# A 3x3 convolution with residual on one core: first image load and first residual load at the fronts of two engines' programs

## The chip, the cores and the metric

The kernel runs on one core of a Trainium2 chip. Its engines are PE (TensorE, matmuls), DVE (VectorE), ACT (ScalarE), POOL (GpSimd) and SP (SyncE, which here only issues DMAs). Each engine runs its own program in order; semaphores tie them together. The metric is the device time of one execution in microseconds (us); a lower time is better.

## The reference

Sixteen images of 64 channels and 64 x 64 pixels, all float32, are convolved with a 64 x 64 x 3 x 3 weight at padding 1, and a residual of the output's shape is added:

```
x_pad = np.pad(x, ((0, 0), (0, 0), (1, 1), (1, 1)))
for b, co, ci, kh, kw:
    output[b, co] += weight[co, ci, kh, kw] * x_pad[b, ci, kh:kh+64, kw:kw+64]
return output + residual
```

## The kernel before

**Data.** Images go in pairs: pair p (0 to 7) is images 2p and 2p+1, whose 128 channels fill the 128 partitions. One load or store of a pair is 128 rows of 16,384 bytes, 2,048 KB. `xr` has three buffers for image pairs as they come from memory, `ro` eight, one for each pair, which take the residual, are added to in place and are stored as the output. `xp` has four buffers for single images in bfloat16, even rows of pixels in partitions 64 to 127 and odd rows in partitions 0 to 63, so that one matmul with 128 rows handles two rows of the kernel at once. `ps` is two PSUM buffers, one image each. `wraw` holds the weights as loaded, 64 rows (output channels) of 2,304 bytes; `wl` holds them transposed, in bfloat16, in the six blocks that the matmuls use.

**The order is written by hand**, an engine at a time:

- SP (L120 to L130) loads, for each pair, the images (`load_x`, L71) and the residual (`load_ro`, L74). From pair 3 on it first waits until ACT has taken the images of the pair three before out of `xr` (L123, semaphore `s_half`). Then it issues five stores (`store`, L77), each once DVE's adds have got so far (L129, `s_add`). All these transfers are on SP's one DMA queue. The last three stores (L217) follow when everything else is done.
- The very first image load is taken out of its place by `to_the_front` (L99) and put into SP's program ahead of the drain at which all engines meet at the start, so it is issued at 0.00.
- ACT issues the load of the weights (L151) on its own DMA queue, and then makes two casts per image from `xr` to `xp` (L159, L163). The first cast of a pair waits for the pair's load.
- POOL writes a 64 x 64 identity for the transposes (L133, L135) and zeros the borders of `xp` and the empty blocks of `wl`.
- PE waits for the identity and the weights (L191, L192), makes nine transposes of 64 x 64 weights into PSUM (L195), one for each position in the 3x3 kernel, and then, for each image, 24 matmuls in six groups of four (L206, recorded at L83 where weights are loaded and L84 where not). Per image it waits for a free PSUM buffer (`s_bank`) and for the image's second cast (`s_pack`).
- DVE waits for the transposes (L166), makes six casts from PSUM into `wl` (L172), and then two adds per image (L182), `ro` = `ps` + `ro`. The first add of a pair waits for the pair's residual (L180: `s_r[p]`, a semaphore for each pair); the first of an image waits for its convolution (`s_conv`). `s_add` rises with an image's first add, so it counts images whose first add is done.

The time from the program's start to the first matmul of L83 therefore takes: the first image load and its casts on one side, the load of the weights, the transposes and DVE's casts on the other.

Of the kernel before, what the change touches and what calls it, by code (L numbers as in the profile page):

```python
# [8 lines left out]
FP32 = mybir.dt.float32  # L9
# [6 lines left out]
def kernel(  # L16
# [7 lines left out]
    nc = tc.nc  # L24
# [6 lines left out]
    NPIX = H * W  # L31
    NPAIR = B // 2
# [3 lines left out]
    NXR = 3  # L36
# [3 lines left out]
    res_bc = residual.rearrange("b c h w -> (b c) (h w)")  # L40
    out_bc = out.rearrange("b c h w -> (b c) (h w)")
    x_bc = x.rearrange("b c h w -> (b c) (h w)")
    w_flat = weight.rearrange("co ci kh kw -> co (ci kh kw)")

    pool = ctx.enter_context(tc.tile_pool(name="pool", bufs=1))
    psum = ctx.enter_context(tc.tile_pool(name="psum", bufs=1, space=bass.MemoryType.PSUM))

    ident = pool.tile([64, 64], FP32)
    ro = [pool.tile([128, NPIX], FP32, name=f"ro{p}") for p in range(NPAIR)]
    xr = [nc.alloc_sbuf_tensor(f"xr{i}", [128, NPIX], FP32) for i in range(NXR)]  # L50

    xp = [pool.tile([128, J + 1, W], BF16, name=f"xp{i}") for i in range(NXP)]
    wraw = nc.alloc_sbuf_tensor("wraw", [64, 576], FP32)
    wl = pool.tile([128, 2, 3, 2, 64], BF16)
    ps = [psum.tile([128, NCHUNK, JC, W], FP32, name=f"ps{i}") for i in range(2)]

    sem = lambda name: tc.alloc_semaphore(name)
    s_w = sem("s_w")
    s_x = [sem(f"s_x{i}") for i in range(NXR)]
    s_r = [sem(f"s_r{p}") for p in range(NPAIR)]  # L60
    s_out = sem("s_out")
    s_id = sem("s_id")
    s_wt = sem("s_wt")
# [4 lines left out]
    s_add = sem("s_add")  # L68

    def load_x(p):  # L70
        return nc.sync.dma_start(out=xr[p % NXR][:, :], in_=x_bc[128 * p : 128 * p + 128, :]).then_inc(s_x[p % NXR], 16)  # L71

    def load_ro(p):
        nc.sync.dma_start(out=ro[p][:, :], in_=res_bc[128 * p : 128 * p + 128, :]).then_inc(s_r[p], 16)  # L74

    def store(p):
        return nc.sync.dma_start(out=out_bc[128 * p : 128 * p + 128, :], in_=ro[p][:, :])  # L77

    def matmul(out_, lhsT, rhs, start, stop, ldweights):

        e = nc.tensor
        if ldweights:
            return e.matmul(out=out_, lhsT=lhsT, rhs=rhs, start=start, stop=stop, skip_group_check=True)  # L83
        return e.add_instruction(  # L84
            mybir.InstMatmult(
                name=nc.get_next_instruction_name(),
                engine=PE,
                ins=[e.lower_ap(rhs), e.lower_ap(lhsT)],
                outs=[e.lower_ap(out_)],
                start_tensor_calc=start,  # L90
                stop_tensor_calc=stop,
                tile_size=(128, 128),
                tile_position=(0, 0),
                bass_skip_group_check=True,
                ldweights=False,
            )
        )

    def to_the_front(dma):  # L99

        def fixed(ap):
            t = ap.bass_ap.tensor.name
            return mybir.PhysicalAccessPattern(
                ap=ap.ap, offset=ap.bass_ap.offset, dtype=ap.dtype, memref=t, memsetref=t + "_set", bass_ap=ap.bass_ap
            )

        front = nc.main_func.blocks[0].instructions
        here = nc.cur_bb.bb.instructions  # L110
        ins = here.pop()
        assert ins.name == dma.ins.name
        at = next(
            i for i, e in enumerate(front) if e.engine == mybir.EngineType.SP and isinstance(e, mybir.InstDrain)
        )
        front.insert(at, copy.replace(ins, ins=[fixed(a) for a in ins.ins], outs=[fixed(a) for a in ins.outs]))

    with tc.tile_critical(no_gpsimd_drain=True):  # L118

        for p in range(NPAIR):  # L120
            if p >= NXR:

                nc.sync.wait_ge(s_half, 2 * (p - NXR) + 3)  # L123
            i = load_x(p)
            if p == 0:
                to_the_front(i)
            load_ro(p)
        for p in range(NEARLY):
            nc.sync.wait_ge(s_add, 2 * p + 3)  # L129
            store(p).then_inc(s_out, 16)  # L130


        nc.gpsimd.memset(ident[:, :], 0.0).then_inc(s_id, 1)  # L133
        nc.gpsimd.wait_ge(s_id, 1)
        nc.gpsimd.affine_select(  # L135
            out=ident[:, :],
            in_=ident[:, :],
            compare_op=mybir.AluOpType.not_equal,
            fill=1.0,
            base=0,  # L140
            pattern=[[-1, 64]],
            channel_multiplier=1,
        ).then_inc(s_id, 1)
        for t in xp:
            nc.gpsimd.memset(t[0:64, 0, :], 0.0).then_inc(s_id, 1)  # L145
            nc.gpsimd.memset(t[64:128, J, :], 0.0).then_inc(s_id, 1)  # L146
        nc.gpsimd.memset(wl[0:64, 0, :, 1, :], 0.0).then_inc(s_id, 1)  # L147
        nc.gpsimd.memset(wl[64:128, 1, :, 0, :], 0.0).then_inc(s_id, 1)  # L148


        nc.scalar.dma_start(out=wraw[:, :], in_=w_flat[:, :]).then_inc(s_w, 16)  # L151
        for n in range(B):
            p, im = divmod(n, 2)
            hp = slice(64 * im, 64 * im + 64)
            x4 = xr[p % NXR].rearrange("q (j two w) -> q j two w", two=2, w=W)
            t = xp[n % NXP]
            if im == 0:
                nc.scalar.wait_ge(s_x[p % NXR], 16 * (p // NXR + 1))
            i = nc.scalar.copy(out=t[64:128, 0:J, :], in_=x4[hp, :, 0, :])  # L159
            i.then_inc(s_half, 1)  # L160
            if n >= NXP:
                i._wait_ge(s_conv, n - NXP + 1)
            nc.scalar.copy(out=t[0:64, 1 : J + 1, :], in_=x4[hp, :, 1, :]).then_inc(s_pack, 1)  # L163


        nc.vector.wait_ge(s_wt, 1)  # L166
        tpf = ps[0].rearrange("p c j w -> p (c j) w")

        blocks = ((0, 0, 0, 0), (1, 0, 0, 1), (1, 0, 1, 0), (0, 1, 0, 2), (0, 1, 1, 1), (1, 1, 1, 2))
        for half, d, par, kh in blocks:  # L170
            hp = slice(64 * half, 64 * half + 64)
            i = nc.vector.tensor_copy(out=wl[hp, d, :, par, :], in_=tpf[0:64, 3 * kh : 3 * kh + 3, :])  # L172
        i.then_inc(s_bank, 2)
        for n in range(B):
            p, im = divmod(n, 2)
            hp = slice(64 * im, 64 * im + 64)
            o4 = ro[p].rearrange("q (j two w) -> q j two w", two=2, w=W)
            psj = ps[n % 2].rearrange("q c j w -> q (c j) w")
            if im == 0:
                nc.vector.wait_ge(s_r[p], 16)  # L180
            for par in range(2):
                i = nc.vector.tensor_tensor(  # L182
                    out=o4[hp, :, par, :], in0=psj[64 * par : 64 * par + 64, :, :], in1=o4[hp, :, par, :], op=ADD
                )
                if par == 0:
                    i._wait_ge(s_conv, n + 1)

                i.then_inc(s_add if par == 0 or n == B - 1 else s_bank, 1)


        nc.tensor.wait_ge(s_id, 4 + 2 * NXP)  # L191
        nc.tensor.wait_ge(s_w, 16)  # L192
        wraw3 = wraw.rearrange("p (ci t) -> p ci t", t=9)
        for t in range(9):
            i = nc.tensor.transpose(out=ps[0][0:64, t // 8, t % 8, :], in_=wraw3[:, :, t], identity=ident[:, :])  # L195
        i.then_inc(s_wt, 1)
        with nc.Fori(0, B // NXP, 1, engines=[PE]):
            for n in range(NXP):
                nc.tensor.wait_ge(s_bank, 1).then_inc(s_bank, -1)
                nc.tensor.wait_ge(s_pack, 1).then_inc(s_pack, -1)  # L200
                order = [(1, 0), (1, 1), (0, 0), (0, 1), (2, 0), (2, 1)]
                for i, (kw, d) in enumerate(order):
                    xlo, xhi = max(0, 1 - kw), min(W, W + 1 - kw)
                    for c in range(NCHUNK):
                        j0 = JC * c
                        m = matmul(  # L206
                            ps[n % 2][:, c, :, xlo:xhi],
                            wl[:, d, kw, :, :].rearrange("q r c -> q (r c)"),
                            xp[n][:, j0 + d : j0 + d + JC, xlo + kw - 1 : xhi + kw - 1],
                            i == 0,  # L210
                            i == len(order) - 1,
                            c == 0,
                        )
                m.then_inc(s_conv, 1)
# [36 lines left out]
```

## Time and profile before

| what | us |
|---|---|
| median of 3 executions | 124.26 (124.14 to 124.42) |
| the profiled execution, its own time | 124.16 |
| its span, first to last instruction | 122.1 |
| PE busy | 86.5 |
| DVE busy | 75.2 |
| ACT busy | 62.0 |
| first cast of ACT starts | 8.89 |
| first cast of image pair 1 starts (image 2) | 18.71 |
| DVE's first add starts | 20.98 |
| SP issues the image loads of pairs 3 to 7 at | 20.63, 30.48, 40.27, 50.06, 59.87 |

Times in the span are counted from its first instruction. The page cuts the span into 40 slices of 3.05 us: a digit is the busy share in tenths, and the row GB/s is what all DMA engines moved. A line of the groups gives the source line, engine, operation, what is written and read, the count, the busy time and the mean duration in ns, and the idle time before with what ended it. A line of the timeline gives the start, the duration, the engine, the line and the count; "q" behind an engine's name is its sequencer, which issues DMAs. A line of the windows gives the stretch, its length, the busy time of PE, weight loads, DVE, ACT and POOL, the granted PE clock, the DMA share and GB/s.

### The profile page before, as it was taken

The page shows a single profiled execution, that of the slowest core. Times are in us where ns is not written, and L with a number is a line of the kernel's source. Part 1 is how long each engine was busy: PE and PEld are TensorE (multiplying, and loading weights), DVE is VectorE, ACT ScalarE, POOL GpSimd, SP SyncE. Part 2 cuts the span into 40 slices and gives each one's busy share as a digit, 9 for nine tenths or more (in the row PEclk, how much of TensorE's full clock was granted, in tenths as well). Part 3 has the DMA queues.
Part 4 walks back from the last instruction along what each step waited for, and adds up shares of the span by engine and source line. Part 5 has one row for each costly group of instructions (what it writes and reads, how often), then busy time and mean ns, then how long its engine had stood idle before and what let it go on. Part 6 is the DMA issues. An engine that isn't in the chain of part 4 may idle for free.

```text
span 122.1 us, 729 instructions
## 1 busy us (share of the span) xinstructions
PE 86.5 (71%) x389; PEld 10.4 (9%) x105; DVE 75.2 (62%) x38; ACT 62.0 (51%) x33; POOL 2.2 (2%) x16
## 2 busy tenths in 40 slices
PE   0003799999999999999999999999999930000000
PEld 0003000101111010101010101111110100000000
DVE  0004101989889898898989889898798988000000
ACT  4009948966984993992994896699000000000000
POOL 5100000000000000000000000000000000000000
PEclk9999999999999999999999999999999999555555
DMA  6999999999999999999999999999999999999993
GB/s 182 408 348 429 429 429 429 429 424 429 429 429 424 429 429 429 429 429 429 429 429 419 429 429 424 429 429 429 435 435 435 429 429 429 435 435 429 429 429 140
DMA packets 3536, 50.48 MB, mean 413 GB/s; under 512 B 400, under 2 KB 400, under 8 KB 464
## 3 DMA queue, kind: packets, MB, share of 16 engines
q1 hardware_dynamic: 3456, 50.33, 97.8%
q10 hardware_dynamic: 80, 0.15, 0.4%
HBM read 33.70 MB, written 16.78 MB: 413 GB/s over the span
## 4 chain that ended last, share of the span: by engine, by line
PE 70%; DVEq 2%; DVE 2%; issue 0%
PE ps L84 53%; PE ps L83 17%; DVEq L118 2%; DVE ro L182 2%
## 5 line engine op out<-in xcount | busy, mean ns | idle before, releaser
L182 DVE TENSOR_TENSOR ro<-ps,ro 64x2048 f32<-64x2048 f32 x32 | 73.2, 2289 | 17.4 <-PE ps L84 16.9
L84 PE MATMUL ps<-xp,wl 128*128 128x504 bf16 (+1 forms) x288 | 79.9, 387 | 0.2
L159 ACT CAST xp<-xr 64x2048 bf16<-64x2048 f32 x16 | 30.3, 1896 | 21.3 <-DMA xr<-in_x_dram 21.1
L83 PE MATMUL ps<-xp,wl 128*128 128x504 bf16 (+1 forms) x92 | 35.6, 387 | 2.4 <-PEq L200 2.4
L163 ACT CAST xp<-xr 64x2048 bf16<-64x2048 f32 x16 | 30.4, 1897 | 0.4
L83 PEld LDWEIGHTS ps<-xp,wl 128*128 128x128 bf16 x96 | 9.5, 99 | 77.5 <-issue 77.5
L172 DVE CAST wl<-ps 64x192 bf16<-64x192 f32 x6 | 1.9, 347 | 10.9 <-PE ps L195 10.8
L195 PE MATMUL ps<-ident,wraw 64*64 64x64 f32 x9 | 1.1, 305 | 9.6 <-DMA wraw<-in_weight_dram 9.6
L159 ACT ACT_TABLE_LOAD x1 | 1.3, 1283 | 1.5 <-SPq L118 1.5
L195 PEld LDWEIGHTS ps<-ident,wraw 64*64 64x64 f32 x9 | 0.9, 163 | 9.6 <-issue 9.6
L146 POOL MEMSET xp<- 64x64 bf16 x4 | 0.6, 147 | 0.2
L145 POOL MEMSET xp<- 64x64 bf16 x4 | 0.6, 145 | 0.2
L148 POOL MEMSET wl<- 64x192 bf16 x1 | 0.3, 253 | 0.1
L147 POOL MEMSET wl<- 64x192 bf16 x1 | 0.3, 252 | 0.1
L135 POOL TENSOR_SCALAR_AFFINE_SELECT ident<-ident 64x64 f32<-64x64 f32 x1 | 0.2, 233 | 0.2 <-POOL ident L133 0.2
L133 POOL MEMSET ident<- 64x64 f32 x1 | 0.1, 145 | 0.5 <-SPq L118 0.5
L235 POOL MEMSET const-bfloat16-1.0<- 128x1 bf16 x1 | 0.1, 113 | 0.0
L235 POOL MEMSET const-uint8-127<- 128x1 uint8 x1 | 0.1, 112 | 0.0
L235 POOL MEMSET const-float32-1.0<- 128x1 f32 x1 | 0.1, 109 | 0.0
L235 POOL MEMSET const-float32-0.0<- 128x1 f32 x1 | 0.1, 104 | 0.2 <-issue 0.2
## 6 DMA issues: line engine op xcount, KB each, us to landing
xr<-in_x_dram SPq DMA_DIRECT2D x8, 2048.0 KB, 17.6
ro<-in_residual_dram SPq DMA_DIRECT2D x8, 2048.0 KB, 22.1
out_dram<-ro SPq DMA_DIRECT2D x8, 2048.0 KB, 28.7
wraw<-in_weight_dram ACTq DMA_DIRECT2D x1, 144.0 KB, 8.5
```

What stands on the lines that cost most here:

```text
L83: return e.matmul(out=out_, lhsT=lhsT, rhs=rhs, start=start, stop=stop, skip_group_check=True)
L84: return e.add_instruction(mybir.InstMatmult(name=nc.get_next_instruction_name(), engine=PE, ins=[e.lower_ap(rhs), e.lower_ap(lhsT)], outs ...
L118: with tc.tile_critical(no_gpsimd_drain=True):
L145: nc.gpsimd.memset(t[0:64, 0, :], 0.0).then_inc(s_id, 1)
L146: nc.gpsimd.memset(t[64:128, J, :], 0.0).then_inc(s_id, 1)
L147: nc.gpsimd.memset(wl[0:64, 0, :, 1, :], 0.0).then_inc(s_id, 1)
L159: i = nc.scalar.copy(out=t[64:128, 0:J, :], in_=x4[hp, :, 0, :])
L163: nc.scalar.copy(out=t[0:64, 1 : J + 1, :], in_=x4[hp, :, 1, :]).then_inc(s_pack, 1)
L172: i = nc.vector.tensor_copy(out=wl[hp, d, :, par, :], in_=tpf[0:64, 3 * kh : 3 * kh + 3, :])
L182: i = nc.vector.tensor_tensor(out=o4[hp, :, par, :], in0=psj[64 * par : 64 * par + 64, :, :], in1=o4[hp, :, par, :], op=ADD)
L195: i = nc.tensor.transpose(out=ps[0][0:64, t // 8, t % 8, :], in_=wraw3[:, :, t], identity=ident[:, :])
L235: nc = _bacc.Bacc("TRN2", target_bir_lowering=False, num_devices=1)
```

## The change

The residual load of pair 0 leaves SP's program and goes to the front of ACT's, ahead of ACT's drain, as the first image load is in SP's. The load of the weights leaves ACT's program; SP issues it in the place where residual 0 was, behind the first image load and on the same queue. The weights now lie as 16 rows of 9,216 bytes (four output channels to a partition), so PE makes 36 transposes of 16 rows by 64 columns, with a 16 x 16 identity. There are three residual semaphores instead of eight; since one is used again for pair p when it was used for pair p-3, SP now waits before the residual load of pair p (3 to 7) until the first add of image 2(p-3) is done. To be addressed ahead of the drain, `ro0` is allocated as `xr` is.

```
-    ident = pool.tile([64, 64], FP32)
-    ro = [pool.tile([128, NPIX], FP32, name=f"ro{p}") for p in range(NPAIR)]
+    ident = pool.tile([16, 16], FP32)
+    ro = [nc.alloc_sbuf_tensor("ro0", [128, NPIX], FP32)]
+    ro += [pool.tile([128, NPIX], FP32, name=f"ro{p}") for p in range(1, NPAIR)]
...
-    wraw = nc.alloc_sbuf_tensor("wraw", [64, 576], FP32)
+    wraw = nc.alloc_sbuf_tensor("wraw", [16, 4, 576], FP32)
...
-    s_r = [sem(f"s_r{p}") for p in range(NPAIR)]
+    s_r = [sem(f"s_r{i}") for i in range(NXR)]
...
-    def load_ro(p):
-        nc.sync.dma_start(out=ro[p][:, :], in_=res_bc[128 * p : 128 * p + 128, :]).then_inc(s_r[p], 16)
+    def load_ro(p, engine=nc.sync):
+        return engine.dma_start(out=ro[p][:, :], in_=res_bc[128 * p : 128 * p + 128, :]).then_inc(s_r[p % NXR], 16)
...
-            i for i, e in enumerate(front) if e.engine == mybir.EngineType.SP and isinstance(e, mybir.InstDrain)
+            i for i, e in enumerate(front) if e.engine == ins.engine and isinstance(e, mybir.InstDrain)
...
             if p == 0:
                 to_the_front(i)
-            load_ro(p)
+                nc.sync.dma_start(out=wraw[:, :, :], in_=w_flat.rearrange("(q u) f -> q u f", u=4)).then_inc(s_w, 16)
+            if p >= NXR:
+
+                nc.sync.wait_ge(s_add, 2 * (p - NXR) + 1)
+            if p > 0:
+                load_ro(p)
...
-            pattern=[[-1, 64]],
+            pattern=[[-1, 16]],
...
-        nc.scalar.dma_start(out=wraw[:, :], in_=w_flat[:, :]).then_inc(s_w, 16)
+        to_the_front(load_ro(0, nc.scalar))
...
-                nc.vector.wait_ge(s_r[p], 16)
+                nc.vector.wait_ge(s_r[p % NXR], 16 * (p // NXR + 1))
...
-        wraw3 = wraw.rearrange("p (ci t) -> p ci t", t=9)
+        wraw4 = wraw.rearrange("q u (ci t) -> q u t ci", t=9)
         for t in range(9):
-            i = nc.tensor.transpose(out=ps[0][0:64, t // 8, t % 8, :], in_=wraw3[:, :, t], identity=ident[:, :])
+            for u in range(4):
+                i = nc.tensor.transpose(
+                    out=ps[0].rearrange("p c j (q u) -> p (c j) u q", u=4)[0:64, t, u, :],
+                    in_=wraw4[:, u, t, :],
+                    identity=ident[:, :],
+                )
```

## The prediction

> **What bounds the kernel now.** I read the page first (engine shares, the 40 slices, the chain), then the windows of half a microsecond over the start, then the timelines of SP, ACT and DVE, and last the end.
>
> ```profile
> DMA  6999999999999999999999999999999999999993
> GB/s 182 408 348 429 429 429 429 429 424 429 429 429 424 429 429 429 429 429 429 429 429 419 429 429 424 429 429 429 435 435 435 429 429 429 435 435 429 429 429 140
> PE 70%; DVEq 2%; DVE 2%; issue 0%
> L195 PE MATMUL ps<-ident,wraw 64*64 64x64 f32 x9 | 1.1, 305 | 9.6 <-DMA wraw<-in_weight_dram 9.6
> ...
> 9.63 1.14 PE L195 MATMUL ps<-ident,wraw 64*64 64x64 f32 x9 [9.63 <-DMA wraw<-in_weight_dram]
> 10.81 1.97 DVE L172 CAST wl<-ps 64x192 bf16<-64x192 f32 x6 [10.81 <-PE ps L195]
> 10.81 1.90 ACT L163 CAST xp<-xr 64x2048 bf16<-64x2048 f32 x1
> 13.12 0.58 PE L83 MATMUL ps<-xp,wl 128*128 128x512 bf16 x1 [2.35 <-PEq L200]
> ...
> 98.78 4.61 DVE L182 TENSOR_TENSOR ro<-ps,ro 64x2048 f32<-64x2048 f32 x2 [0.58 <-PE ps L84]
> 103.68 1.76 SPq L77 DMA_DIRECT2D out_dram<-ro  x3
> ```
>
> The DMA engines never rest, and the chain of waits runs almost wholly over PE: two bounds, nearly equal. The DMA side: 50.48 MB at 429 GB/s is 117.7 us. Of this the loads, the weights and the first five stores (44.2 MB) take 103 us; counting bytes to 10 us in the windows, the stream behaves as if it ran at full rate from about 2.4 us, so they are done near 105.3. The compute side: PE starts at 13.12, the first image takes 7.86 us (DVE's first add starts at 20.98), the other fifteen 5.19 each without a gap, DVE adds 4.61 behind the last, and SP issues the last three stores at 103.68. An issue at time 0.0 had its first packets between 1.0 and 1.5, so with an empty queue these stores would start at about 104.9. Compute therefore has 0 to 0.6 us of slack; I use 0.3. Any later start of PE by more than that goes to the end one for one.
>
> The start of PE hangs on two chains that are equal: x0 lands 8.89, two ACT copies, 12.71; weights land 9.45 (issue 0.95 plus 8.5), transposes 9.63 to 10.77, six DVE casts to 12.78, PE 13.12.
>
> How two DMA queues share is visible at the start, where the weights are the only transfer on ACT's queue:
>
> ```profile
> 1.00:1.50 0.50, 0.00 (x0) 0.00 (x0) 0.00 (x0) 0.00 (x0) 0.27 (x2) 1.00 2.50 492
> 1.50:2.00 0.50, 0.00 (x0) 0.00 (x0) 0.00 (x0) 0.48 (x1) 0.39 (x4) 1.00 0.12 33
> ...
> 5.00:5.50 0.50, 0.00 (x0) 0.00 (x0) 0.00 (x0) 0.00 (x0) 0.00 (x0) 1.00 1.11 472
> 5.50:6.00 0.50, 0.00 (x0) 0.00 (x0) 0.00 (x0) 0.00 (x0) 0.00 (x0) 1.00 0.83 332
> 7.00:7.50 0.50, 0.00 (x0) 0.00 (x0) 0.00 (x0) 0.00 (x0) 0.00 (x0) 1.00 0.71 224
> 8.00:8.50 0.50, 0.00 (x0) 0.00 (x0) 0.00 (x0) 0.00 (x0) 0.00 (x0) 1.00 0.69 239
> ```
>
> The last column is GB/s. A packet of a big load is one 16,384 B row (128 per load, 8 per engine), one of the weights a 2,304 B row (64, 4 per engine). A window's bytes then split into packets: 426 GB/s for 0.5 us is 13 big ones; 472 is 13 big and 10 small, 332 is 9 and 8, 224 is 5 and 13, 239 is 7 and 2. Split so, all seven windows from 5.0 to 8.5 us hold 10, 8, 11, 11, 13, 9, 2 small packets, 64 in all: every weight packet, about one for one with big ones. So the queues take turns packet by packet, after a lead of some five packets per engine that were taken before the weights came. An engine starts a packet every 0.615 us (13 per 0.5 us over 16), the first one taking about 1.3.
>
> [...] the nine pairs here come every 103 ns (0.93/9). [...] Here PE matmuls are slow (1.70 us per four instead of 0.86) for the 5.06 us from 13.12 to 18.18.
>
> **The change, part by part.**
>
> *Residual 0 to the front of ACT's program.* It was 8 packets per engine behind x0 on the same queue; now it starts with x0 on another queue and takes every second turn. x0's eighth packet was turn 8 (with some small weight packets between) and is now turn 15. With the second turn starting at 2.55 (1.25 + 1.3), turn 15 starts at 2.55 + 13 x 0.615 = 10.5. Landing follows a packet's start by 1.4 to 1.9 (x0: 7.0 to 8.89), so x0 lands near 12.4 instead of 8.9. The bounds: SP's load ahead by the five packets seen, then it is turn 11, landing 9.9; ACT's ahead, turn 16, landing 13.0. No row shows which front runs first, so I take equal arrival. ACT's image 0 copies then end at 12.4 + 3.82 = 16.2. The issue itself (0.53 us on ACT) leaves the place before the table load, which is over long before x0 comes.
>
> *Weights on SP, behind x0.* One issue in the place of residual 0's (0.99, about 0.4). On the queue they are behind eight packets of x0 and still beside residual 0: turn 17, starting 2.55 + 15 x 0.615 = 11.8, landing about 13.4 (bounds 11.2 with SP ahead[...]). Before: 9.45. Sixteen rows of 9,216 B replace 64 small ones: the three windows from 7.0 to 8.5 moved 449 KB where 644 (429 GB/s) would fit, so the small packets cost 0.45 us beyond their bytes, and about 0.4 may come back. It is on the DMA side, which will not be the bound. x1's issue stands behind one issue on SP now and then.
>
> *36 transposes instead of 9.* Each 64 columns against 16: [...] 103 (the present pitch, if pairs have a floor). I take 75: 35 x 0.075 + 0.305 for the last = 2.93 us instead of 1.14. It is on the path, since PE waits for weights. Then 0.04 and the same six casts 1.97 and 0.34 to PE's first matmul.
>
> *Sum.* 13.4 + 0.18 + 2.93 + 0.04 + 1.97 + 0.34 = 18.86. PE started at 13.12: 5.74 later. x0's chain, 16.2, now waits for the weights. Minus 0.3 of slack: +5.44. Span 122.1 + 5.44 = 127.5; the profiled execution's own time was 124.16, 2.06 above its span, so 129.6; the median is 0.10 above that execution: 129.7.
>
> *Edits at nothing.* The smaller identity: POOL is done at 3.71, PE waits for weights far longer. Three residual semaphores instead of eight, and their waits on SP: residual p (3 to 7) now waits for the first add of image 2(p-3). Those adds end at 23.27, 33.64, 44.02, 54.39, 64.77 now, so 29.0 to 70.5 with PE 5.74 late. The queue needs residual p when x of p has been moved, some 2 us before its landing (ACT's copies start 38.35, 48.14, 57.95, 67.73, 77.53): 36.3 to 75.5. Margin 7.3 falling to 5.0, less 1.2 for an issue to reach the engines. Queued behind each wait on SP are the next x load, whose own wait ends about as late, and from residual 7 on the stores: the first four go at about 71 instead of from 60.7, while loads last to 80. Cover is gone if PE starts about 9.5 us late. x1 and later loads keep their place in the byte stream (x1 landed 18.71, about the same after), and PE needs image 2 ten microseconds later than that.
>
> **Rivals.** A, the forecast: fair turns, 129.7.
> B: SP's x0 gets the lead of five packets that the weights' late start shows. x0 lands 9.9, weights 11.2; PE starts 16.7, 3.5 late; +3.2, 127.5. For it: SP's issue is the first instruction of the span. Against: ACT's front is not seen, and both stand at the program's head.
> C: [...] All of the cold phase is worth 5.06/2 = 2.5 us; half of it on A gives about 128.4. [...]
> D: ACT's queue ahead[...], 103 ns per transpose[...]; 131.8 to 132.
> E, the other side[...]: if the weights land before 10.2 (13.12 + 2.53 - 5.46), [...] the DMA side decides, shorter by 0.4: 123.8. For it: landing at 9.6 is possible if residual 0 hardly mixes with x0. Against: the mix seen[...].
>
> **How the numbers follow.** A 0.55, B 0.25, C 0.08, D 0.08, E 0.04. Range 126.8[...] to 132.0. About 0.2% (0.25 us) is what a measurement of this kernel can tell from no change: faster 0.04, same 0.02, slower 0.94.
>
> **What would show it.** x0's first ACT copy at 12 to 13 instead of 8.89; transposes starting near 13.6, x36, lasting near 3 us; PE's first matmul near 19; DVE's first add near 26.7; the last three stores near 109.4; and a hole of about 4 us in the DMA row before them, after a full row until then. Wrong if x0 still lands near 9, if the transposes overlap x0's copies, or if holes appear in the DMA row before 100 us (then the new waits cost).

## The result and the profile after

The changed kernel takes 128.41 us (median of 6, 127.17 to 129.09) beside 124.23 of the kernel before in the same runs: ratio 1.0312, 95% interval 1.0256 to 1.0369. The ratio leaves out the execution of 129.09, more than 1.5% above the fastest one, and sets a mean of 128.17 against 124.29. The forecast was 129.7 with a range of 126.8 to 132.0. The execution profiled took 129.06, its span is 126.4; before, 124.16 and 122.1.

The page of the changed kernel, the same rows as before: DMA share and GB/s in 40 slices (3.16 us each now), the chain by engine, and the group of the transposes.

```profile
DMA  7999899999999999999999999999999994199994
GB/s 239 420 420 368 342 430 436 441 425 420 420 430 436 441 425 420 420 430 436 430 436 420 420 430 425 436 441 420 425 430 436 441 420 176 83 415 415 420 477 181
PE 68%; DVEq 2%; DVE 2%; issue 0%
L202 PE MATMUL ps<-ident,wraw 16*64 16x16 f32 x36 | 2.3, 214 | 14.2 <-DMA wraw<-in_weight_dram 14.2
```

Two things are new in the DMA rows: a dip in the fourth and fifth slices (368 and 342 GB/s, 9.5 to 15.8 us), and a hole in the slices that read 176 and 83. In the hole nothing is left to move: the loads and the first five stores are done and the last three have not reached the engines (no packet of data starts between 105.6 and 110.2 us). In the kernel before there was no such hole. The compute side now sets the end.

The timeline of the changed kernel gives the chain that does it (start, duration, engine, line):

```profile
0.00 0.39 SPq L72 DMA_DIRECT2D xr<-in_x_dram  x1
0.12 0.36 ACTq L75 DMA_DIRECT2D ro<-in_residual_dram  x1
1.12 0.35 SPq L128 DMA_DIRECT2D wraw<-in_weight_dram  x1
...
11.60 1.90 ACT L165 CAST xp<-xr 64x2048 bf16<-64x2048 f32 x1 [9.24 <-DMA xr<-in_x_dram]
14.21 2.27 PE L202 MATMUL ps<-ident,wraw 16*64 16x16 f32 x36 [14.21 <-DMA wraw<-in_weight_dram]
16.52 1.97 DVE L178 CAST wl<-ps 64x192 bf16<-64x192 f32 x6 [16.52 <-PE ps L202]
18.79 0.58 PE L84 MATMUL ps<-xp,wl 128*128 128x512 bf16 x1 [2.30 <-PEq L211]
...
26.67 4.61 DVE L188 TENSOR_TENSOR ro<-ps,ro 64x2048 f32<-64x2048 f32 x2 [8.17 <-PE ps L85]
...
109.37 1.77 SPq L78 DMA_DIRECT2D out_dram<-ro  x3
```

The first image load lands at 11.60 instead of 8.89, and its two casts end at 15.4. The weights land only at 14.1, so the transposes begin 4.58 us later than before, take 2.27 instead of 1.14, and PE's first real matmul comes at 18.79 instead of 13.12: 5.67 later. From there nothing has changed. The last three stores are issued at 109.37 instead of 103.68, 5.69 later.

The end is only 4.3 later, because the tail has become shorter. By the tail I mean the time from the issue of those stores to the end of the span: it is 126.4 - 109.37 = 17.03 us now, with an empty queue, and it was 122.1 - 103.68 = 18.42, with earlier transfers still moving. So the kernel before had 1.4 us of slack on its compute side. In the five traces of variants below in which the compute side also decides, the tail is 17.0 to 17.1 too.

Where the stream dips, the windows of the changed kernel read as follows (last column GB/s):

```profile
11.00:11.50 0.50, 0.00 (x0) 0.00 (x0) 0.00 (x0) 0.00 (x0) 0.00 (x0) 1.00 0.62 264
11.50:12.00 0.50, 0.00 (x0) 0.00 (x0) 0.00 (x0) 0.40 (x1) 0.00 (x0) 1.00 2.83 490
12.00:12.50 0.50, 0.00 (x0) 0.00 (x0) 0.00 (x0) 0.50 (x1) 0.00 (x0) 1.00 0.57 98
12.50:13.00 0.50, 0.00 (x0) 0.00 (x0) 0.00 (x0) 0.50 (x1) 0.00 (x0) 1.00 0.27 66
13.00:13.50 0.50, 0.00 (x0) 0.00 (x0) 0.00 (x0) 0.50 (x1) 0.00 (x0) 1.00 0.67 229
13.50:14.00 0.50, 0.00 (x0) 0.00 (x0) 0.00 (x0) 0.48 (x1) 0.00 (x0) 1.00 0.79 328
```

A packet is counted where it starts, so 490 followed by 98 and 66 means that the engines all took up a packet and then sat on it: in the packet records of this trace the big packets that start between 11.5 and 12 us last 1.50 to 1.69 us instead of 0.61. Over 11 to 14 us they moved 246 GB/s on average; at 429 that stretch would have lasted (429 - 246)/429 x 3 = 1.28 us less. I call such a figure the loss of a stretch; it holds no bytes of the weights, since these are in the rate. Before, over 5 to 8.5 us, where the weights moved, the loss was (429 - 360)/429 x 3.5 = 0.56:

```profile
5.00:8.50 3.50, 0.00 (x0) 0.00 (x0) 0.00 (x0) 0.00 (x0) 0.00 (x0) 1.00 1.02 360
```

How the two big loads of the changed kernel shared the engines is in its packets, counted by queue: q1 is SP's, q10 ACT's, and a line gives the packets, the MB and the share of the 16 engines. First from 1 to 2.5 us, then from 2.5 to 10:

```profile
q1 hardware_dynamic: 29, 0.48, 101.7%
...
q1 hardware_dynamic: 99, 1.62, 50.4%
q10 hardware_dynamic: 96, 1.57, 49.5%
```

x0 alone moves at first, about two packets on each engine; residual 0, though issued at 0.12, starts its first packet at 2.62. From then on the two take equal turns. x0's last packet starts at 9.99, residual 0's at 11.21, and only then the weights' 16 rows start, from 11.32 to 11.82.

### The profile page after: what moved, and what is told of

Read it like the earlier page. It is cut to its first block, busy times and chain, and to the rows that moved or that the text cites. A ratio compares the mean times of both kernels' runs of the same rounds, so it can differ in the third digit from the quotient of the medians.

```text
span 126.4 us, 787 instructions
## 1 busy us (share of the span) xinstructions
PE 87.9 (70%) x420; PEld 11.7 (9%) x132; DVE 75.2 (59%) x38; ACT 62.0 (49%) x33; POOL 2.1 (2%) x16
## 4 chain that ended last, share of the span: by engine, by line
PE 68%; DVEq 2%; DVE 2%; issue 0%
PE ps L85 51%; PE ps L84 17%; DVEq L119 2%; DVE ro L188 2%
## 5 line engine op out<-in xcount | busy, mean ns | idle before, releaser
L85 PE MATMUL ps<-xp,wl 128*128 128x504 bf16 (+1 forms) x288 | 79.9, 387 | 0.0
L84 PE MATMUL ps<-xp,wl 128*128 128x504 bf16 (+1 forms) x96 | 37.2, 387 | 2.3 <-PEq L211 2.3
L202 PE MATMUL ps<-ident,wraw 16*64 16x16 f32 x36 | 2.3, 214 | 14.2 <-DMA wraw<-in_weight_dram 14.2
L202 PEld LDWEIGHTS ps<-ident,wraw 16*64 16x64 f32 x36 | 2.2, 149 | 14.2 <-issue 14.2
```

What stands on the lines that cost most here:

```text
L85: return e.add_instruction(mybir.InstMatmult(name=nc.get_next_instruction_name(), engine=PE, ins=[e.lower_ap(rhs), e.lower_ap(lhsT)], outs ...
L202: i = nc.tensor.transpose(out=ps[0].rearrange("p c j (q u) -> p (c j) u q", u=4)[0:64, t, u, :], in_=wraw4[:, u, t, :], identity=ident[:, :],)
```

## Experiments

Each ratio is to the kernel before in the same runs.

**Which part makes the weights late.** The changed kernel with residual 0 taken back to SP's queue:

```
-            if p > 0:
-                load_ro(p)
+            load_ro(p)
...
-        to_the_front(load_ro(0, nc.scalar))
```

> The changed kernel with residual 0 back on SP's queue, behind the weights; all else as changed. Theory (the two big loads take turns, and the weights wait for both): x0 has the engines to itself again, ACT's first copy near 8.9 (11.60 in the changed kernel); the weights are turn 9, so the transposes start near 9.5 to 10.5 (14.21); PE's first matmul near 14.5 (18.79); the time then falls to 124 to 125.5, where the DMA side decides. Rival (the weights are late because of their own shape or queue, not because of residual 0): transposes stay near 13 to 14, PE near 18, time 127.5 to 128.5.

125.14 us, ratio 1.0092 (1.0057 to 1.0126). In its timeline the casts start at 8.58, the transposes at 9.69 and PE at 14.28:

```profile
9.69 2.29 PE L200 MATMUL ps<-ident,wraw 16*64 16x16 f32 x36 [9.69 <-DMA wraw<-in_weight_dram]
14.28 0.59 PE L84 MATMUL ps<-xp,wl 128*128 128x512 bf16 x1 [2.31 <-PEq L209]
```

One load on another queue therefore moves the weights by 4.5 us (14.21 to 9.69) and PE's start by 4.5. Of the roughly 4 us that the change costs, about 3 go with it (3.3 by the medians, 2.7 by the ratios). The rival, that the weights are late by their own shape or queue, falls: both are as in the changed kernel here.

**What makes the dip.** If it is the 16 rows, it goes with them. The changed kernel with the weights in their old form, 64 rows, nine transposes:

```
...
-    wraw = nc.alloc_sbuf_tensor("wraw", [16, 4, 576], FP32)
+    wraw = nc.alloc_sbuf_tensor("wraw", [64, 576], FP32)
...
```

> The changed kernel with the weights in the old form, 64 rows of 2,304 B, the 64 x 64 identity and nine transposes, in the new place on SP's queue. Theory[...]: the hole shrinks from about 1.3 us to 0.5 or less, the weights land 0.5 to 1 earlier, the transposes take 1.14 instead of 2.27; PE's first matmul near 16.8 (18.79); time near 126.5. Rival (the hole comes from the hand-over of the two queues, when both big loads end together): it stays at 1 us or more between 11.5 and 14, the weights land near 14, PE near 17.6; time near 127.3.

126.50 us, ratio 1.0185 (1.0167 to 1.0203). The loss over 11 to 14 us halves, to (429 - 339)/429 x 3 = 0.63; transposes start at 13.27 and PE at 16.76:

```profile
11.00:14.00 3.00, 0.73 (x8) 0.76 (x9) 0.00 (x0) 2.54 (x2) 0.00 (x0) 1.00 0.97 339
```

The second half of the prediction's chain is measured by this: the form of the weights costs 2.0 us of PE's start, 0.9 by their landing and 1.1 by the transposes.

And the form alone, in the kernel before, in the weights' old place on ACT's queue:

> The kernel before with only the weights' form changed: 16 rows, 16 x 16 identity, 36 transposes, in their old place on ACT's queue. Theory (the hole belongs to the 16 rows): the windows between 4 and 9 us lose about 1.3 us of transfer, 0.8 more than the 0.45 of the kernel before; PE's first matmul near 14.2 (13.12); the DMA side is later by 0.8; time near 125.0. Rival (no hole from the form; fewer, larger rows are cheaper): no loss in the windows, PE near 14, time 123.7 to 124.2.

125.73 us, ratio 1.0112 (1.0086 to 1.0138), more than expected; of the 1.4 us only 0.9 lies in the span (123.0 against 122.1), the rest outside it, as the last section tells. PE starts at 13.83 and the last stores are issued at 103.87, so the compute side would end at 103.87 + 17.03 = 120.9; the span is 123.0. It is the DMA stream that is late. The windows of this run, the 4 us in which the weights move:

```profile
5.00:9.00 4.00, 0.00 (x0) 0.00 (x0) 0.00 (x0) 0.00 (x0) 0.00 (x0) 1.00 1.00 254
```

The loss is (429 - 254)/429 x 4 = 1.63 us, with no second big load on another queue that could end at the same time. The rival of the run before (a hand-over of queues) falls with this.

**Partitions or packets.** Sixteen rows are fewer and longer packets, and they go to 16 partitions. To part the two, the kernel before got a second, unused load of the weights in 16 rows, once into partitions 0 to 15 and once into every fourth partition up to 60:

```
+        nc.scalar.dma_start(out=wx[0:16, :], in_=w_flat.rearrange("(q u) f -> q (u f)", u=4)).then_inc(s_dum, 16)
```
```
+        nc.scalar.dma_start(out=wx[0:64:4, :], in_=w_flat.rearrange("(q u) f -> q (u f)", u=4)).then_inc(s_dum, 16)
```

> The kernel before with a second load of the weights, unused, on ACT's queue behind the first: 16 rows of 9,216 B into partitions 0 to 15[...]. Both theories: the DMA stream loses 1.1 to 1.6 us beyond the bytes (0.34 us), time 125.7 to 126.2.

> As the run with the extra 16 rows, but into partitions 0, 4, 8 to 60[...], same rows, same packets. Theory[...]: about half the loss, 0.5 to 0.8 us beyond the bytes, time 125.0 to 125.5. Rival (the size or number of the packets, or 16 engines with one row each): the same loss as with partitions 0 to 15, 125.7 to 126.2.

126.23 us, ratio 1.0167 (1.0143 to 1.0192), and 124.89, ratio 1.0054 (1.0033 to 1.0076). The same 147 KB in the same 16 rows cost 2.05 us and 0.71. Without the 0.34 us of the bytes at full rate that is 1.71 and 0.37 beyond them. The windows say much the same; first the run with partitions 0 to 15, then the other:

```profile
5.00:12.00 7.00, 1.14 (x9) 0.93 (x9) 0.73 (x3) 2.78 (x2) 0.00 (x0) 1.00 1.02 302
```
```profile
5.00:12.00 7.00, 1.14 (x9) 0.93 (x9) 0.76 (x3) 3.08 (x2) 0.00 (x0) 1.00 1.01 365
```

Losses of 2.07 and 1.04 us, where the kernel before has 0.59 over the same stretch (393 GB/s): 1.48 and 0.45 more. So the partitions decide, and not the number or length of the rows; by what mechanism, the runs do not show. The big loads are held up too: their packets that start beside the extra rows, from 8.5 to 9.5 us, last 1.35 to 1.65 us with the first set and 0.84 to 1.04 with the second, where 0.61 is usual.

**The new waits on SP.** The changed kernel with eight residual semaphores and without the five waits on `s_add`:

```
...
-            if p >= NXR:
-
-                nc.sync.wait_ge(s_add, 2 * (p - NXR) + 1)
...
```

> The changed kernel with eight residual semaphores as before and without SP's waits ahead of the residual loads. Theory (these waits are covered by a full queue): PE starts at the same time, the last three stores are issued at the same time, time within 0.7 of the changed kernel's 128.4. Rival (the waits cost, by loads or stores that come late): time lower by 1 or more, 127.4 or less, with stores starting at 60 instead of 71.

128.72 us (127.79 to 128.75), ratio 1.0336 (1.0294 to 1.0379), beside 1.0312 of the changed kernel. SP issues residual 3 at 21.44 instead of 28.98 and the stores from 60.80 instead of 70.84, and PE starts at 18.80 as with the waits. They cost nothing that can be measured here; the two intervals overlap, and each is over 1 us wide.

**Weights ahead of x0, residual 0 still beside it.**

```
+            if p == 0:
+                to_the_front(nc.sync.dma_start(out=wraw[:, :, :], in_=w_flat.rearrange("(q u) f -> q u f", u=4)).then_inc(s_w, 16))
             i = load_x(p)
             if p == 0:
                 to_the_front(i)
-                nc.sync.dma_start(out=wraw[:, :, :], in_=w_flat.rearrange("(q u) f -> q u f", u=4)).then_inc(s_w, 16)
...
```

> The changed kernel with the weights' load (16 rows) moved to the front of SP's program, ahead of the first image load; residual 0 stays at ACT's front. A second, small read of the weights at the end of ACT's program (16 KB) is added, which nothing uses. Theory (the changed kernel's delay is the weights' chain, and x0's chain lies hidden 3 us behind it): transposes start before 6, x0 lands near 12 to 13, and now x0's two ACT copies set PE's start, near 16.2 to 17; time 126 to 127. Rival (x0's late landing is already what binds): PE's start stays near 18.8, time near 128.4.

127.56 us, ratio 1.0275 (1.0248 to 1.0302): neither. The weights are there at 4.86, but x0 now lands at 14.17 instead of 11.60, and PE, waiting for x0's casts, starts at 18.13:

```profile
4.86 2.28 PE L206 MATMUL ps<-ident,wraw 16*64 16x16 f32 x36 [4.86 <-DMA wraw<-in_weight_dram]
18.13 0.59 PE L86 MATMUL ps<-xp,wl 128*128 128x512 bf16 x1 [10.99 <-PEq L215]
```

In both kernels the same three transfers share the first stretch, and the one that stands last on SP's queue lands at about 14.2: the weights there, x0 here. With residual 0 beside them, the exchange of the other two only chose which chain was late. I had taken x0's landing as if the weights in front of it cost nothing; with them it lands 2.6 us later. The packets show where: the weights' rows start by 1.35, residual 0's packets from 1.44, and x0's first only at 5.26, when 59 of residual 0's 128 have gone.

**The weights at ACT's front.** The kernel before, with only that:

```
-        nc.scalar.dma_start(out=wraw[:, :], in_=w_flat[:, :]).then_inc(s_w, 16)
+        to_the_front(nc.scalar.dma_start(out=wraw[:, :], in_=w_flat[:, :]).then_inc(s_w, 16))
...
```

> The kernel before with its weights' load (64 rows) at the front of ACT's program; everything else as before, with a small unused read of the weights (16 KB) at the end of ACT's program. Theory (in the kernel before the DMA side decides, with 1.4 us of slack on the compute side, and its first microsecond has room): the weights move while the first packets of x0 are under way, the loss at 5 to 8.5 us goes, and the whole stream ends 0.3 to 0.8 earlier: 123.4 to 123.9. Rival (compute decides, or the weights now take turns from x0): x0 lands 0.5 or more later than 8.9 and the time is unchanged or higher, 124.2 to 124.8.

124.20 us, ratio 1.0002 (0.9990 to 1.0013). A miss: issued at 0.13 instead of 0.95, the weights let the transposes start at 9.24 instead of 9.63; their first row starts at 4.60 instead of 5.21. An earlier issue on a second queue bought 0.4 us of 0.8, and nothing of the time.

**x0 on two queues.** Its columns halved, one half at each front, and then the same with the weights in 32 rows:

```
+                for h, e in enumerate((nc.sync, nc.scalar)):
+                    hf = slice(NPIX // 2 * h, NPIX // 2 * h + NPIX // 2)
+                    to_the_front(e.dma_start(out=xr[0][:, hf], in_=x_bc[0:128, hf]).then_inc(s_x[0], 16))
...
```

> The kernel before with its first image load cut in two by columns (128 rows of 8,192 B each), one half at the front of SP's program, one at the front of ACT's; residual 0 and the weights as before. Theory (the second queue fills the DMA engines' first two microseconds, as residual 0 did in the changed kernel: 29 packets of 16 KB started by 2.5 us instead of 20, and this time both queues carry x0): x0 lands 0.2 to 0.4 earlier than 8.9, the DMA stream, which decides, ends 0.2 to 0.4 earlier, time 123.8 to 124.0. Rival (smaller packets lose it again, or the start is bound otherwise): 124.2 or more.

> As the run with x0 on two queues, and the weights as 32 rows of 4,608 B ([...]half as many packets), a 32 x 32 identity and 18 transposes. Theory: the weights' loss of DMA time halves from 0.45, another 0.1 to 0.3; PE's start within 0.5 of 13.1; time 123.6 to 123.9. Rival[...]: as the run with x0 on two queues.

125.70 us, ratio 1.0123 (1.0106 to 1.0139), and 124.52, ratio 1.0025 (1.0009 to 1.0041). The theory fails: x0 lands at 9.15 and 8.79, hardly changed from 8.89, and the weights, now behind half of x0 on ACT's queue, land late, so that PE starts at 16.81 and 15.26. The packets of the first run show why they come 4 us later than before, with only half a load ahead of them: that half takes turns with SP's queue, first with the other half and then with rows of residual 0, twice as long. Its last packet starts at 7.83, and the weights' rows follow from 8.94 to 11.83 (5.21 to 8.13 in the kernel before). The theory also rested on a misreading: the 29 packets that the changed kernel had started by 2.5 us were all x0's own, none of residual 0.

**A weights' form between the two.** 32 rows of 4,608 B, half as many packets as with 64 rows, and 18 transposes, in the old place:

```
...
-    wraw = nc.alloc_sbuf_tensor("wraw", [64, 576], FP32)
+    wraw = nc.alloc_sbuf_tensor("wraw", [32, 2, 576], FP32)
...
```

> The kernel before with the weights as 32 rows of 4,608 B, 32 x 32 identity and 18 transposes, all else as before. Theory[...]: the time stays within 0.2 of 124.2. Rival (the form itself costs, in proportion to the rows' length): halfway to the run with 16 rows alone, 125.0.

123.80 us, ratio 0.9976 (0.9967 to 0.9984): a little faster than the kernel before, where I had expected no change. The rival, a cost that grows with the rows' length, is out. The gain doesn't come from the stretch in which the weights move: from 1 to 12 us both kernels move 372 GB/s. From 12 to 100 us this one moves 431 and the kernel before 429, which is 0.4 us; why is open.

Then the same 32 rows ahead of x0, both at the front of SP's program, with residual 0 behind them on the same queue:

> The kernel with 32 weight rows, and these ahead of the first image load, both at the front of SP's program (a small unused read of the weights, 4 KB, is added at the end of ACT's program). Theory ([...]small rows there cost less than later, and x0 is alone behind them): weights land before 5, x0 lands 9.2 to 9.6, PE starts 13.3 to 13.8, inside the compute side's slack; the DMA stream ends up to 0.3 earlier: 123.5 to 123.8. Rival (the front of the queue is as dear as any place, or dearer): 123.8 to 124.5.

123.27 us (123.18 to 123.48), ratio 0.9925 (0.9911 to 0.9939): it beats both kernels, and by more than was expected. Its timeline:

```profile
0.00 0.39 SPq L127 DMA_DIRECT2D wraw<-in_weight_dram  x1
0.45 0.41 SPq L73 DMA_DIRECT2D xr<-in_x_dram  x1
...
4.17 1.26 PE L200 MATMUL ps<-ident,wraw 32*64 32x32 f32 x18 [4.17 <-POOL wl L152]
12.26 0.58 PE L85 MATMUL ps<-xp,wl 128*128 128x512 bf16 x1 [6.82 <-PEq L209]
```

The transposes wait for POOL's zeros now and no longer for the weights. x0 is issued 0.45 later than before and yet lands earlier, at 8.30 instead of 8.89, although its last packet starts no earlier (7.21, before 7.15). What differs is that no packet is held up: of the big packets that start between 4 and 14 us none lasts over 0.62 us here, where 45 last over 0.7 in the kernel before. The windows from 1 to 12 us, first the kernel before, then this one:

```profile
1.00:12.00 11.00, 1.14 (x9) 0.93 (x9) 1.16 (x4) 4.37 (x3) 1.99 (x12) 1.00 1.00 372
...
1.00:12.00 11.00, 1.26 (x18) 1.13 (x18) 1.93 (x6) 4.96 (x3) 1.94 (x12) 1.00 1.01 392
```

That is (392 - 372)/429 x 11 = 0.5 us. The span is 121.1, 1.0 shorter; the other half gathers later, as in the run before this one, and is as open. Why small rows at the front hold nothing up, the runs do not show.

## Why the prediction was right

It was right in its chain and its bound; the terms that were off, against what was measured:

- *Fair turns.* x0 at 12.4 predicted, 11.60 measured (11.43 and 11.47 in two other runs with residual 0 beside it): between the equal turns that were chosen and the 9.9 of the lead. Giving residual 0 back its place brings 8.58. The turns were equal, but after a lead of about two packets per engine (29 in all by 2.5 us) for SP's queue; the forecast had none, rival B five.
- *Weights.* Their rows were predicted to start at 11.8 and start from 11.32 to 11.82. They were to land at about 13.4; they land at 14.1, and the transposes, predicted for 13.6, start at 14.21. The surplus goes with the 16 rows: with the old form the transposes start at 13.27. The forecast's own sum had no such surplus; that 16 rows might land later than 64 was a guess at the upper end of its range, which no trace of the kernel before showed. The expected gain of 0.4 us of DMA time was a loss in the weights' stretch, 1.28 us instead of 0.56. Over 1 to 14 us the two streams are still nearly level (376 GB/s, before 381), since the changed kernel moved more by 2.5 us.
- *Transposes.* 2.93 us predicted, 2.27 measured, or (2.27 - 0.21)/35 = 59 ns for each pair of weight load and matmul. The 75 ns of the forecast was a guess: the kernel before shows only pairs with 64 moving columns, at 103 ns (0.93 us for nine).
- *PE's start.* 18.86 predicted, 18.79 measured. That it is so close is luck: the transposes start 0.6 us later than forecast and take 0.7 us less, and the two cancel.
- *Slack.* This is the term that was mis-sized: 0.3 us taken, 0 to 0.6 allowed, 1.4 measured. The time at which the earlier transfers are done was right (105.3; the packets of the last three stores start from 105.43). Two things were not. With an empty queue the first packet starts 0.84 us after the issue (110.21 against 109.37, and 0.83 or 0.84 in five variants), where 1.25 had been taken from the issue at time 0.0, so these stores could have started at 104.5: 0.9 us of slack. And from their first packet to the end of the span an empty queue needs 16.18 us, where the kernel before took 16.66; the forecast had no such term. Together this explains the 1.1 us between the span predicted, 127.5, and the 126.4 measured. The median is 1.3 below the forecast. That the profiled execution came closer (129.06, predicted 129.6) is luck again: it spent 2.66 us outside its span where 2.06 had been taken.
- *Waits and identity at nothing.* Shown for the waits: 128.72 without them. The identity was not tried alone.
- *PE's slow phase.* The forecast let it stay as it was. It lasts 5.07 us (18.79 to 23.86; before 5.06), and image 0, from the first matmul to DVE's first add, takes 26.67 - 18.79 = 7.88 us, before 7.86. One pair of traces proves little, since image 0 varies from trace to trace. But in the four traces with 36 transposes that end 2.3 us before the first matmul it takes 7.34 to 8.11, and in six with nine transposes 6.67 to 8.32: no gain of the 1.3 us or so that rival C forecast. That the longer transposes would shorten this phase, as C and E had it, was a guess that no run showed.

Of the signs that the prediction named the late ones came as written: DVE's first add at 26.67, the last stores at 109.37, a hole of over 4 us before them. An early one did not: x0's first copy was to come at 12 to 13 and came at 11.60. Rival E's condition was weights before 10.2 us. The changed kernel with residual 0 back on SP's queue met it (9.69) without winning anything back: image 0 took 8.1 us. The run with 32 rows ahead of x0 met it and won, but by an earlier x0 and less DMA time, and not by a shorter image 0, which took 20.57 - 12.26 = 8.31 us.

## What to carry to other kernels

When two big loads start together on two queues, the one that everything waits for no longer has the engines to itself (x0 landed at 11.60 us beside residual 0 and at 8.58 without it); give the second queue something that isn't the rival of the first, or put the transfers on one queue in the order in which they are needed. A small load goes ahead of a big one on the same queue when a chain hangs on it (with nothing big beside it, 32 rows ahead of x0 gave 123.27 us beside 124.23; with residual 0 at ACT's front that order helped little here, 127.56 beside 128.41). Which partitions it goes to is worth a trial: 16 rows cost 1.71 us beyond their bytes in partitions 0 to 15, and 0.37 in every fourth up to 60. Before pricing a delay, measure the tail from the last issue to the end, since the slack is what is left of it.

## What the runs showed of the hardware

- 147 KB into partitions 0 to 15 took 1.71 us of the whole DMA stream beyond its bytes; into every fourth partition up to 60 it took 0.37.
- A transfer on a second queue did not start moving when it was issued. Beside an x0 issued at 0.00, weights issued at 0.13 started their first row at 4.60 and landed at about 9.2, and a residual issued at 0.12 started at 2.62. Ahead of x0 on the same queue the weights (32 rows) started at 1.02 and were there by 4.2.
- Part of the time lies outside the span. In eleven of the fourteen traces the execution's own time is 2.0 to 2.1 us above its span. In three, the changed kernel, the 16 rows alone and the weights ahead of x0, it is 2.6 to 2.8, and in just these three a packet of 16 KB of kind "instruction" moves after the span's end (at 128.14 us in the changed kernel). Executions without a trace show it too: those of the five kernels with 36 transposes lie 2.0 to 3.1 us above their spans, all others 2.0 to 2.2. That the packet is the cause is not shown, nor why only some executions have it.
- The changed kernel's executions differ by 1.9 us and those of the kernel before by 0.4; 1.5 us of the 1.9 are in the spans (125.1 to 126.6). Image 0, in which PE's slow phase lies, took between 6.67 and 8.32 us in the fourteen traces, while from DVE's first add to the issue of the last stores all of them took 82.7. A range of that size would cover the spread of the spans in a kernel whose compute side decides, and 1.4 us of slack would hide it in the kernel before. With one trace for each kernel this fits, but is not shown.
